# Hybrid decoder step on one core: projection stripes in another order, four projection banks, key rows turned by VectorE

## The chip, the cores and the metric

The kernel runs on one core of one Trainium2 chip. The metric is device time in microseconds, from the first to the last instruction of one execution with what lies around it; a smaller time is better. Times of before are of three runs, and one further execution was taken with the hardware profiler.

## What is computed

One layer of a decoder trunk is run on 1024 new prompt tokens and on 8 sampled tokens with caches, 1032 columns in all. Model width is 1024.

```python
xn = rms_norm(x, norm_pre)
u, z_rnn, q, k, v, z_attn, g_rnn, g_attn = split(xn @ w_in)       # 1024 -> 9216 columns
uc, conv_new = causal_conv(u, conv_buf, conv_w, conv_b)           # 4 taps
r, i = sigmoid(uc @ lru_w_a + b_a), sigmoid(uc @ lru_w_x + b_x)   # blocks of 64
a = exp(-8 * r * softplus(-lam))
h = scan(h = a * h + sqrt(1 - a * a) * i * uc)                    # over the tokens
y_rnn = (h * silu(z_rnn)) @ w_rnn_out
# three groups (window, dilation) = (128, 1), (512, 4), (2048, 16), 8 heads of 64 each
o_g, lse_g = dilated windowed attention with ALiBi per group      # sampled tokens read caches
y_attn = (merge of o_g by softmax(lse_g) * silu(z_attn)) @ w_attn_out
y = x + rms_norm((sigmoid(g_rnn) * y_rnn + sigmoid(g_attn) * y_attn) @ w_out, norm_post)
```

Outputs are y for both kinds of tokens, the convolution's and the recurrence's states, and the rows of k and v that the caches keep: of the prompt the last 128, 512 and 1024 positions of the three groups, for each of them 8 heads of 64 numbers.

## The kernel before

All products with weights are made of three passes in fp32r: each operand is split into a high part and a rest (`whi`, `wlo` and `xh`, `xl`; ScalarE makes the high part by a copy, VectorE the rest by a subtraction, L225 and L226), and `mm3` (L389) adds high x high, high x low, low x high. The normalised input lies in SBUF as 8 + 8 tiles [128, 1032]. `w_in` is used in 72 stripes of 128 columns, each loaded whole by SP (512 KB, L207). One stripe is one call of `project` (L409): three chunks of 256, 384 and 392 columns, each with 8 x 3 matmuls into a PSUM bank of the tag `pj`, which has two banks; then an eviction. The tags `s` (three banks), `pt` (two) and `o` (one) serve everything else.

Evictions: `proj_u` (L534) copies by ScalarE; `proj_z` (L545) and `proj_za` (L682) take Sigmoid by ScalarE and multiply by VectorE; `proj_g` (L1105) takes Sigmoid by ScalarE and then stores the tile to DRAM, after which its slot is free.

SBUF tiles come from `Arena`: 42 slots of one [128, 1059] tile, handed out first in, first out. If none is free, `get` calls `force`, which runs steps of the background lanes at once, whether due or not, until one is.

Work beside the projections stands in generators in lanes (`lru`, `attention`, `sample`, `merge`). The program is written out in one order by a planner: `clk` counts the price of each PE instruction, `mm` (L138) charges it, and a generator yields the time after which it may go on. `advance` runs a stripe and calls `tick` after each half chunk; `tick` issues at most one step of each lane that is due. A lane runs its generators one after the other.

The recurrence is four chains (`chain`, L611), two 128-row blocks each, all in the lane `lru`. A chain's front (`chain_front`, L561) does the convolution, splits the result and makes the gates: 12 steps of two matmuls and two activations per chain, 1300 apart (L603). Then Tanh into a new tile, Exp, Sqrt, VectorE work, the scan (L641), and the product with z, which is stored.

Order of the stripes: the first four (u0 to u3) are computed in four chunks (`EARLY`), interleaved by hand (`half`, `turned`) with the normalisation of the four token groups, whose transposed tiles they need; the norm takes a Sqrt on ScalarE per group (L335). Then z0 to z3, u4, u5, z4, z5, u6, u7, z6, z7, four za stripes and six gate stripes. A chain starts when both its u stripes and its z stripes are done, except that the first starts with z0. Then for each of four pairs of heads and each of three groups v, k, q, after which `attention` (L788) and, per pair, `sample` (L966) are spawned. The remaining ten gate stripes run under the last attention; two stripes before their end all merged heads and samples must have been issued (`until`, L1223). Three output products follow.

In `attention`, six steps, `STEP` apart, per group and pair. At the third and fourth step `k_rows` (L766) turns the kept 128-column blocks of k (1, 4 or 8 of them) by PE transposes into a bank `s`, copies them out by VectorE (L779), and later stores them: `store_rows` (L735) writes one row of 128 numbers per token, 512 bytes a piece.

## Time and profile before

| | |
|---|---|
| median of three runs | 1291.03 us (1291.01 to 1292.82) |
| the profiled execution's own time | 1294.25 us |
| its span, first to last instruction | 1292.5 us |
| mean granted TensorE clock | 0.987 |
| PE busy | 1258.5 us, 97% |
| VectorE (DVE), ScalarE (ACT), GpSimd (POOL) busy | 604.6, 553.2, 221.9 us |
| DMA moved | 125.98 MB, 32% of 16 queues' time |

The engines work side by side, each in its own order; one instruction waits until what it reads is written and what it overwrites is read. Busy PE means that a matmul is under way; matmuls overlap, so the lengths of single ones add up to more than their time. The granted clock is a share of the full 2.4 GHz.

### The profile page before, as it was taken

The page shows a single profiled execution, that of the slowest core. Times are in us where ns is not written, and L with a number is a line of the kernel's source. Part 1 is how long each engine was busy: PE and PEld are TensorE (multiplying, and loading weights), DVE is VectorE, ACT ScalarE, POOL GpSimd, SP SyncE. Part 2 cuts the span into 40 slices and gives each one's busy share as a digit, 9 for nine tenths or more (in the row PEclk, how much of TensorE's full clock was granted, in tenths as well). Part 3 has the DMA queues.
Part 4 walks back from the last instruction along what each step waited for, and adds up shares of the span by engine and source line. Part 5 has one row for each costly group of instructions (what it writes and reads, how often), then busy time and mean ns, then how long its engine had stood idle before and what let it go on. Part 6 is the DMA issues. An engine that isn't in the chain of part 4 may idle for free.

```text
span 1292.5 us, 21498 instructions
## 1 busy us (share of the span) xinstructions
PE 1258.5 (97%) x8726; PEld 1209.8 (94%) x8726; DVE 604.6 (47%) x1323; ACT 553.2 (43%) x1231; POOL 221.9 (17%) x232
## 2 busy tenths in 40 slices
PE   8999999799999999999999999999999999999997
PEld 8999998789999989999999999999999999998997
DVE  5552472761574274544256324643345245554226
ACT  6536636445539744334334344333652331222222
POOL 5000221311220131150026001420026000002001
PEclk9999999899999999999999999999999999998999
DMA  7210130232330133632074016512365474223115
GB/s 234 67 33 17 33 99 17 71 125 69 100 112 5 49 96 108 165 84 66 17 212 120 25 42 164 135 50 66 97 189 154 137 260 150 66 66 99 33 67 197
DMA packets 149449, 125.98 MB, mean 97 GB/s; under 512 B 8873, under 2 KB 135305, under 8 KB 149342
## 3 DMA queue, kind: packets, MB, share of 16 engines
q1 hardware_dynamic: 149350, 124.61, 32.0%
q8 instruction: 69, 1.13, 0.4%
q14 instruction: 30, 0.25, 0.1%
HBM read 98.44 MB, written 26.21 MB: 96 GB/s over the span
## 4 chain that ended last, share of the span: by engine, by line
PE 87%; ACT 5%; DVE 5%; issue 1%; DMA 1%; POOL 0%; SPq 0%; DVEq 0%; ACTq 0%
PE ps_pj L146 75%; PE ps_s L146 5%; PE ps_o L146 3%; PE ps_s L150 3%; PE ps_pt L150 2%; ACT gate L601 1%; DVE wlo L226 1%; DVE tanh L641 1%; ACT whi L225 1%; DMA wraw<-in_w_in 1%; DVE ck L1057 1%; ACT gate L623 1%; ACT sq L627 0%; ACT P L823 0%; ACT L627 0%
## 5 line engine op out<-in xcount | busy, mean ns | idle before, releaser
L146 PE MATMUL ps_pj<-xh,whi 128*128 128x256 f32 (+3 forms) x1760 | 574.7, 327 | 12.1 <-DVE za L687 11.0
L146 PE MATMUL ps_pj<-xl,whi 128*128 128x256 f32 (+3 forms) x1760 | 560.4, 318 | 0.0
L146 PE MATMUL ps_pj<-xh,wlo 128*128 128x256 f32 (+3 forms) x1760 | 560.1, 318 | 0.0
L146 PEld LDWEIGHTS ps_pj<-xh,whi 128*128 128x128 f32 x1760 | 334.0, 190 | 21.0 <-DVE za L687 12.4
L146 PEld LDWEIGHTS ps_pj<-xl,whi 128*128 128x128 f32 x1760 | 334.0, 190 | 0.2
L146 PEld LDWEIGHTS ps_pj<-xh,wlo 128*128 128x128 f32 x1760 | 333.6, 190 | 0.0
L226 DVE TENSOR_TENSOR wlo<-wraw,whi 128x512 fp32r<-128x512 f32 x176 | 149.6, 852 | 320.0 <-ACT whi L225 314.0
L225 ACT ACTIVATE whi<-wraw 128x512 fp32r<-128x512 f32 x176 | 109.6, 625 | 3.9 <-DMA wraw<-in_w_in 1.9
L823 ACT ACTIVATE P<-P,stat 128x128 f32<-128x128 f32 (+1 forms) x192 | 84.3, 440 | 53.0 <-DVE stat L819 52.9
L146 PE MATMUL ps_pj<-wlo,mh 128*128 128x256 f32 (+1 forms) x288 | 80.6, 286 | 0.1
L146 PE MATMUL ps_pj<-whi,mh 128*128 128x256 f32 x256 | 73.3, 286 | 2.7 <-ACT whi L225 2.7
L146 PE MATMUL ps_pj<-whi,ml 128*128 128x256 f32 x256 | 73.2, 286 | 0.0
L716 ACT ACTIVATE qt<-ps_pj,qsc 128x384 f32<-128x384 f32 (+1 forms) x36 | 27.6, 766 | 81.5 <-PE ps_pj L146 79.6
L146 PE MATMUL ps_pj<-hzh,wlo 128*128 128x256 f32 (+2 forms) x192 | 61.4, 320 | 0.0
L146 PE MATMUL ps_pj<-hzl,whi 128*128 128x256 f32 (+2 forms) x192 | 61.4, 320 | 0.0
L146 PE MATMUL ps_pj<-hzh,whi 128*128 128x256 f32 (+2 forms) x192 | 61.3, 319 | 0.0
L1109 ACT ACTIVATE sg<-ps_pj 128x256 f32<-128x256 f32 (+2 forms) x48 | 22.0, 458 | 91.7 <-PE ps_pj L146 90.4
L819 DVE CUSTOM_DVE_ANT_0 P<-ps_s,base 128x128 f32<-128x128 f32 (+1 forms) x192 | 56.0, 348 | 8.5 <-PE ps_s L146 8.0
L840 ACT ACTIVATE PT<-ps_pt 128x256 f32<-128x256 f32 (+1 forms) x48 | 21.0, 437 | 91.0 <-PE ps_pt L150 90.9
L601 ACT ACTIVATE gate<-ps_s,par 64x256 f32<-64x256 f32 (+2 forms) x96 | 52.1, 543 | 16.0 <-PE ps_s L146 14.4
L838 DVE COPY PT<-ps_pt 128x512 f32<-128x512 f32 (+1 forms) x48 | 28.7, 597 | 54.1 <-PE ps_pt L150 54.1
L146 PEld LDWEIGHTS ps_pj<-wlo,mh 128*128 128x128 f32 (+1 forms) x288 | 52.3, 181 | 0.5 <-DVE wlo L226 0.4
(247 smaller groups left out, 1690.1 us busy)
## 6 DMA issues: line engine op xcount, KB each, us to landing
wraw<-in_w_in SPq DMA_DIRECT2D x72, 512.0 KB
ck<-in_cache_kv_w SPq DMA_DIRECT2D x24, 512.0 KB
sgd<-sg SPq DMA_DIRECT2D x16, 516.0 KB
sgl<-sgd SPq DMA_DIRECT2D x16, 516.0 KB
xin<-in_x_prompt SPq DMA_DIRECT2D x16, 512.0 KB
qb<-sd SPq DMA_DIRECT2D x12, 512.0 KB
fb<-fd SPq DMA_DIRECT2D x24, 256.0 KB
hzd<-uc SPq DMA_DIRECT2D x8, 516.0 KB
```

What stands on the lines that cost most here:

```text
L146: nc.tensor.matmul(out, lhsT, rhs, start=start, stop=stop)
L150: nc.tensor.transpose(out, in_, idn)
L225: nc.scalar.activation(hi[:, a:b], raw[:, a:b], AF.Copy)
L226: nc.vector.tensor_tensor(lo[:, a:b], raw[:, a:b], f32(hi[:, a:b]), op=OP.subtract)
L601: nc.scalar.activation(G[gate][rows, cs], p[at:at + 64, :n], AF.Sigmoid, bias=par[rows, b, 5 + gate:6 + gate])
L623: nc.scalar.activation(R[b], R[b], AF.Exp, scale=spk[:, 1, b:b + 1])
L716: nc.scalar.activation(dst, src, AF.Copy, scale=C["qsc"][:, g, hp:hp + 1])
L819: nc.vector.tensor_tensor_reduce(out=pt[:, h, :128 * n], in0=ps[h][:, off:off + 128 * n], in1=base, scale=-SLOPES[g][2 * hp + h] * DIL[g], ...
L823: nc.scalar.activation(pt[:, h, :128 * n], pt[:, h, :128 * n], AF.Exp, scale=-1.0, bias=st[:, g, 0, h, b:b + 1], accum_out=st[:, g, 1, h, ...
L838: nc.vector.tensor_copy(t, src)
L840: nc.scalar.activation(t, src, AF.Copy)
L1109: nc.scalar.activation(z[:, c0:c0 + n], p[:, :n], AF.Sigmoid)
```

## The change

The 28 early stripes (u, z, za and now eight gates) come in a new order, and the chains start with the second u of their pair; eight gate stripes remain late. While the early stripes and the last two gate stripes and everything behind run, the banks of the tag `pt` serve the projections too, in turn with `pj`. The planner charges n / 2.25 + 4 for an fp32r matmul. The gate steps are 1000 apart, and Tanh is written over the input gate's tile. `k_rows` turns the kept blocks of k by one VectorE transpose of 32x32 squares in place of PE transposes and copies, at the third step; a square row holds 32 numbers, so the store, four DMAs per tile, writes pieces of 128 bytes.

```diff
--- before.py
+++ after.py
@@ -24,13 +24,18 @@
 WIN = (128, 512, 2048)
 COL_U, COL_Z, COL_Q, COL_K, COL_V = 0, 1024, 2048, 3584, 5120
 COL_ZA, COL_GR, COL_GA = 6656, 7168, 8192
-UZ = ((COL_U, (0, 1, 2, 3)), (COL_Z, (0, 1, 2, 3)), (COL_U, (4, 5)), (COL_Z, (4, 5)), (COL_U, (6, 7)), (COL_Z, (6, 7)))
 EPS = 1e-6
 BIG = 1e30
 NSLOT = 42
 WARM = 40
-EARLY_GATES = 6
 GATES = [(kind, b) for kind in range(2) for b in range(8)]
+LATE_GATES = 8
+
+FIRST = [("u", 0), ("u", 1), ("g", 0), ("g", 1)]
+EARLY_BLOCKS = [("z", 0), ("z", 1), ("u", 2), ("u", 3), ("g", 2), ("g", 3),
+                ("z", 2), ("z", 3), ("u", 4), ("u", 5), ("g", 4), ("g", 5),
+                ("z", 4), ("z", 5), ("u", 6), ("u", 7), ("g", 6), ("a", 0),
+                ("z", 6), ("z", 7), ("a", 1), ("a", 2), ("a", 3), ("g", 7)]
 STEP = 3400
 SPARE = 5
 KY, VY = 3000, 4000
@@ -78,7 +83,13 @@
     ar = Arena(arena_pool, NSLOT)
     new = ar.get
 
+
+    wide, turns = [True], [0]
+
     def ps_tile(tag):
+        if tag == "pj" and wide[0]:
+            turns[0] += 1
+            tag = ("pj", "pj", "pt", "pt")[turns[0] % 4]
         bufs = {"pj": 2, "s": 3, "pt": 2, "o": 1}[tag]
         return psum.tile([128, 512], F32, tag=tag, bufs=bufs, name="ps_" + tag)
 
@@ -140,7 +151,7 @@
         for q in out.shape[1:]:
             n *= q
         if rhs.dtype == F32R:
-            clk[0] += n / 2.4 if n >= 256 else max(4 * n / 2.4, 107)
+            clk[0] += n / 2.25 + 4 if n >= 256 else max(4 * n / 2.4, 107)
         else:
             clk[0] += max(4 * n / 2.4, 214) * (0.75 if out.shape[0] == 64 else 1.0)
         nc.tensor.matmul(out, lhsT, rhs, start=start, stop=stop)
@@ -171,19 +182,19 @@
     w_ao = I["w_attn_out"][0].rearrange("(k p) c -> p k c", p=128)
     w_oo = I["w_out"][0].rearrange("(k p) c -> p k c", p=128)
     WL = []
-    for base, bl in UZ:
-        for b in bl:
-            WL.append(w_in[:, :, base + 128 * b:base + 128 * b + 128])
-    for hp in range(4):
-        WL.append(w_in[:, :, COL_ZA + 128 * hp:COL_ZA + 128 * hp + 128])
-    for kind, b in GATES[:EARLY_GATES]:
-        WL.append(w_in[:, :, (COL_GA, COL_GR)[kind] + 128 * b:][:, :, :128])
+    for what, i in FIRST + EARLY_BLOCKS:
+        if what == "g":
+            kind, b = GATES[i]
+            c = (COL_GA, COL_GR)[kind] + 128 * b
+        else:
+            c = {"u": COL_U, "z": COL_Z, "a": COL_ZA}[what] + 128 * i
+        WL.append(w_in[:, :, c:c + 128])
     for hp in range(4):
         for g in range(3):
             for base in (COL_V, COL_K, COL_Q):
                 c = base + g * 512 + hp * 128
                 WL.append(w_in[:, :, c:c + 128])
-    for kind, b in GATES[EARLY_GATES:]:
+    for kind, b in GATES[-LATE_GATES:]:
         WL.append(w_in[:, :, (COL_GA, COL_GR)[kind] + 128 * b:][:, :, :128])
     for s in range(4):
         WL.append(w_ao[:, :, 256 * s:256 * s + 256])
@@ -600,13 +611,12 @@
                     at = 64 * (gate ^ s)
                     nc.scalar.activation(G[gate][rows, cs], p[at:at + 64, :n], AF.Sigmoid,
                                          bias=par[rows, b, 5 + gate:6 + gate])
-                yield 1300
+                yield 1000
         ar.free(*xs)
         R[b], gi = G
         nc.gpsimd.tensor_tensor(x, x, gi, op=OP.mult)
-        t = T[b] = new([128, NT], F32, "tanh")
-        nc.scalar.activation(t, R[b], AF.Tanh, scale=spk[:, 0, b:b + 1])
-        ar.free(gi)
+        T[b] = gi
+        nc.scalar.activation(gi, R[b], AF.Tanh, scale=spk[:, 0, b:b + 1])
 
     def chain(j):
         bl = (2 * j, 2 * j + 1)
@@ -763,25 +773,34 @@
             step = bl[1] - bl[0] if len(bl) > 1 else 1
             later(3000, lambda: store_rows(g, hp, 1, vn[:, bl[0]:8:step], bl))
 
-    def k_rows(g, hp, i):
+    def k_rows(g, hp):
+
         bl = kept(g)
-        part = bl[4 * i:4 * i + 4]
-        if not part:
-            return
+        n = len(bl)
         kt = kts[g, hp]
-        if i == 0:
-            kns[g, hp] = new([128, len(bl), 128], F32, "kn")
-        kn = kns[g, hp]
-        p = ps_tile("s")
-        for q, b in enumerate(part):
-            tr(p[:, 128 * q:128 * q + 128], kt[:, 128 * b:128 * b + 128], ident)
-        n = len(part)
-        nc.vector.tensor_copy(kn[:, 4 * i:4 * i + n], p[:, :128 * n].rearrange("p (b c) -> p b c", b=n))
-        if 4 * i + n == len(bl):
-            def out():
-                store_rows(g, hp, 0, kn, bl)
-                ar.free(kns.pop((g, hp)))
-            later(3000, out)
+        kn = kns[g, hp] = new([128, n, 4, 32], F32, "kn")
+        step = bl[1] - bl[0] if n > 1 else 1
+        nc.vector.transpose(kn.rearrange("p b c j -> p b (c j)"),
+                            kt.rearrange("p (b x) -> p b x", x=128)[:, bl[0]:8:step])
+        o = kv_out[g]
+        off = o.offset + hp * 128
+
+        def out():
+            for a in range(4):
+                src = kn[32 * a:32 * a + 32]
+                at = off + 32 * a
+                if g == 0:
+                    ap, src = [[1024, 32], [32768, 4], [1, 32]], src[:, 0]
+                elif g == 1:
+                    ap = [[4096, 32], [1024, n], [131072, 4], [1, 32]]
+                    at += (bl[0] // 2) * 1024
+                else:
+
+                    ap = [[16384, 32], [1024, 2 * n], [524288, 2], [1, 32]]
+                    src = src.rearrange("p b (r c) j -> p (b r) c j", r=2)
+                nc.sync.dma_start(bass.AP(tensor=o.tensor, offset=at, ap=ap), src)
+            ar.free(kns.pop((g, hp)))
+        later(3000, out)
 
     stats = {}
 
@@ -875,8 +894,8 @@
                 values(pairs[i - 2])
             if i < 2:
                 v_rows(g, hp, i)
-            elif i < 4:
-                k_rows(g, hp, i - 2)
+            elif i == 2:
+                k_rows(g, hp)
             if i == 3:
                 ar.free(kts.pop((g, hp)), qts.pop((g, hp)))
             if i == 5:
@@ -1102,12 +1121,12 @@
 
     sgd = dram.tile([2, KB, 128, NT], F32, name="sgd")
 
-    def proj_g(kind, b):
+    def proj_g(kind, b, chunks=CHUNKS):
         z = new([128, NT], F32, "sg")
 
         def evac(c0, n, p):
             nc.scalar.activation(z[:, c0:c0 + n], p[:, :n], AF.Sigmoid)
-        yield from project(evac)
+        yield from project(evac, chunks)
 
         def spill():
             nc.sync.dma_start(sgd[kind, b], z)
@@ -1137,7 +1156,7 @@
     def turned(gi, k0=0):
         ahead[:] = [lambda k: k >= k0 and next(norm[gi], None)]
 
-    started = [proj_u(b, EARLY) for b in range(4)]
+    started = [proj_u(0, EARLY), proj_u(1, EARLY), proj_g(*GATES[0], EARLY), proj_g(*GATES[1], EARLY)]
 
     def half(i, n=1):
         for _ in range(n):
@@ -1189,20 +1208,12 @@
     clear_low_w()
     C = late_consts()
     spawn("lru", chain(0))
-    for b in range(4):
-        advance(proj_z(b))
-    spawn("lru", chain(1))
-    for j in (2, 3):
-        for b in (2 * j, 2 * j + 1):
-            advance(proj_u(b))
-        for b in (2 * j, 2 * j + 1):
-            advance(proj_z(b))
-        spawn("lru", chain(j))
+    for what, i in EARLY_BLOCKS:
+        advance({"u": proj_u, "z": proj_z, "a": proj_za}[what](i) if what != "g" else proj_g(*GATES[i]))
+        if what == "u" and i % 2:
+            spawn("lru", chain(i // 2))
     spawn("lru", state_out())
-    for hp in range(4):
-        advance(proj_za(hp))
-    for kind, b in GATES[:EARLY_GATES]:
-        advance(proj_g(kind, b))
+    wide[0] = False
     for hp in range(4):
         for g in range(3):
             for kind in (2, 1, 0):
@@ -1218,11 +1229,12 @@
         nc.sync.dma_start(t, sgd[kind, b])
         sgt[kind, b] = t
 
-    for i, (kind, b) in enumerate(GATES[EARLY_GATES:]):
-        if i == len(GATES) - EARLY_GATES - 2:
+    for i, (kind, b) in enumerate(GATES[-LATE_GATES:]):
+        if i == LATE_GATES - 2:
             until(lambda: len(merged) == 4 and len(sampled) == 4)
             spawn("split", split_ya())
-        if i == len(GATES) - EARLY_GATES - 3:
+            wide[0] = True
+        if i == LATE_GATES - 3:
             load_sg(0, 0)
             load_sg(0, 1)
         advance(proj_g(kind, b))
```

## Rows read from the trace of the kernel before

**Rows 1.** The profile's page: busy us, share, instructions of each engine.

```profile
PE 1258.5 (97%) x8726; PEld 1209.8 (94%) x8726; DVE 604.6 (47%) x1323; ACT 553.2 (43%) x1231; POOL 221.9 (17%) x232
```

**Rows 2.** Windows: start:end, length, busy (instructions) by engine, PEclk, DMA, GB/s.

```profile
160.00:192.00 32.00, 32.00 (x206) 32.00 (x206) 23.34 (x28) 11.63 (x21) 9.76 (x13) 1.00 0.33 100
192.00:224.00 32.00, 29.32 (x171) 27.95 (x170) 8.97 (x13) 20.46 (x37) 2.38 (x2) 0.95 0.06 17
224.00:256.00 32.00, 25.10 (x146) 24.37 (x144) 21.90 (x19) 15.42 (x20) 12.51 (x7) 0.89 0.21 64
256.00:288.00 32.00, 27.89 (x162) 27.25 (x163) 21.88 (x30) 12.73 (x21) 6.93 (x11) 0.95 0.39 135
288.00:320.00 32.00, 32.00 (x202) 32.00 (x201) 4.39 (x7) 17.76 (x35) 1.12 (x1) 1.00 0.14 50
```

**Rows 3.** Timeline of ACT: start, length, operation, count, idle before.

```profile
211.08 1.17 ACT L601 ACTIVATE gate<-ps_s,par 64x384 f32<-64x384 f32 x2 [1.28 <-PE ps_s L146]
...
213.62 9.13 ACT L601 ACTIVATE gate<-ps_s,par 64x392 f32<-64x392 f32 x16
```

**Rows 4.** Timeline of ACT: starts of recurrence chains, fourth chain's Sqrt.

```profile
72.56 1.27 ACT L573 ACTIVATE cv<-ext,par 128x1056 f32<-128x1056 f32 x1
...
175.36 1.27 ACT L573 ACTIVATE cv<-ext,par 128x1056 f32<-128x1056 f32 x1 [0.78 <-POOL ext L570]
...
362.26 1.27 ACT L573 ACTIVATE cv<-ext,par 128x1056 f32<-128x1056 f32 x1 [5.96 <-POOL ext L570]
...
448.77 2.02 ACT L627 ACTIVATE sq<-tanh 128x1032 f32<-128x1032 f32 x2
```

**Rows 5.** Windows around the fourth chain's Exp and Sqrt.

```profile
452.00:456.00 4.00, 2.42 (x14) 2.09 (x12) 4.00 (x13) 1.26 (x1) 0.00 (x0) 1.00 0.00 0
456.00:460.00 4.00, 3.14 (x20) 1.81 (x22) 3.62 (x9) 2.22 (x11) 1.16 (x1) 0.86 0.24 70
460.00:464.00 4.00, 4.00 (x31) 3.67 (x28) 2.77 (x9) 2.32 (x9) 1.21 (x1) 0.71 0.00 1
```

**Rows 6.** Lines by form: count, busy us, mean ns of one.

```profile
L641 DVE TENSOR_TENSOR_SCAN tanh<-gate,sq 128x1024 f32<-128x1024 f32 x8 | 27.1, 3391 | 0.0
...
L150 PE MATMUL ps_s<-ident,kt 128*128 128x128 f32 x52 | 9.7, 301 | 0.0
...
L633 DVE TENSOR_SCALAR gate<-tanh 128x1032 f32<-128x1032 f32 x8 | 7.6, 946 | 0.1
```

**Rows 7.** Timeline of PE: a series of eight transposes.

```profile
402.51 1.04 PE L150 MATMUL ps_pt<-ident,P 128*128 128x128 f32 x8
```

**Rows 8.** Windows of 2 us: recurrence weight loads; one key store.

```profile
38.00:40.00 2.00, 2.00 (x20) 2.00 (x19) 1.72 (x4) 1.63 (x4) 0.00 (x0) 1.00 0.43 97
...
464.00:466.00 2.00, 2.00 (x16) 2.00 (x15) 1.16 (x2) 0.94 (x2) 0.00 (x0) 1.00 0.46 129
```

**Rows 9.** Timelines of SP and ACT: a weight load, its conversion.

```profile
506.65 3.25 SPq L207 DMA_DIRECT2D wraw<-in_w_in  x1
...
537.23 0.62 ACT L225 ACTIVATE whi<-wraw 128x512 fp32r<-128x512 f32 x1
```

**Rows 10.** Timelines of ACT and PE at the start.

```profile
32.55 0.20 ACT L335 ACTIVATE rstd<-rstd 128x2 f32<-128x2 f32 x1 [0.90 <-DVE rstd L334]
...
59.31 1.28 ACT L504 ACT_TABLE_LOAD   x1
...
24.67 0.38 PE L146 MATMUL ps_pj<-xh,whi 128*128 128x256 f32 x1 [0.56 <-ACT ext L540]
...
35.19 0.38 PE L150 MATMUL ps_s<-ident,xin 128*128 128x128 f32 x2
```

**Rows 11.** Timelines of ACT and DVE in the late gates.

```profile
927.64 0.50 ACT L1109 ACTIVATE sg<-ps_pj 128x392 f32<-128x392 f32 x1 [0.25 <-PE ps_pj L146]
...
997.40 0.50 ACT L1109 ACTIVATE sg<-ps_pj 128x392 f32<-128x392 f32 x1 [8.01 <-PE ps_pj L146]
...
992.40 0.17 DVE L1068 TENSOR_TENSOR ys<-ys,zas 128x8 f32<-128x8 f32 x1
```

## The prediction

> **What bounds the kernel now.** I read the page first, then the span in windows, then the timelines of the windows that stand out. TensorE (PE) is busy for 97% of the span and VectorE and ScalarE for less than half [rows 1]. So only three things can move the end: matmuls that are no longer issued, idle time of PE, and time in which PE runs at the lower (1.2 GHz) of its two clock levels. The total hides where the idle time lies, so I cut the span into windows of 32 us. In the stage of the input projections a clean window holds 206 or 202 matmuls. Three neighbouring windows, 192 to 288 us, hold 171, 146 and 162, with PE busy for 29.32, 25.10 and 27.89 us and a granted clock of 0.95, 0.89 and 0.95 [rows 2]. The shapes are those of the clean windows, so the count measures the loss: three windows at the mean of 204 would hold 612, there are 479, and 133 / 204 x 32 = 20.9 us are gone. This is the largest hole behind the start.
>
> The timeline of ScalarE says what made it. The recurrence's gates are normally two activations at a time with a piece of projection between, as at 211.08. At 213.62 sixteen come without a break, 9.13 us [rows 3], so eight steps of the recurrence were issued back to back. The code has one reason for that: `new` found no free slot and pumped the background lanes. The count agrees. Of 42 slots 16 hold xh and xl and 2 the recurrence weights, and the weights of two blocks take 5 at least and 7 when loads run ahead, so 17 to 19 are left. At 213 us the second chain holds 10 (x, two split copies and two gates for each of two blocks), stripes u4 to u7 four, z2 to z7 six: 20 before the first za tile is asked for. The lane was then pressed through its VectorE part as well, and every eviction queued behind it.
>
> A second, smaller loss lies where the fourth chain's Exp and Sqrt fall between the attention's Exp: PE is busy for 2.42 and 3.14 of 4 us and the clock falls to 0.86 and 0.71 [rows 5]. That is 1.58 + 0.86 of idle time and 0.14 x 4 + 0.29 x 4 = 1.7 of clock, 4.2 us.
>
> **The order of the stripes.** The chains run one behind the other: 102.8 us lie between the start of the first and of the second (72.56 to 175.36), and the fourth starts at 362.26 [rows 4]. In the new order u and z of a pair come when a chain can use them, with gate stripes between, which need their slot only until their store. I count the new worst case: a chain in its gates 10, the next pair's u two, its own z two, the following z one or two, one gate or za tile waiting for its store: 16 or 17, against the 20 of before and 17 to 19 available. So the forced run goes, and its 20.9 us with it. With a chain running at its ordinary pace the clean windows show PE busy for 32.00 of 32 us with two banks [rows 2], so nearly nothing should remain; I leave 0.5. Gain **20.4 us**; bounds 10 (the lane is still pressed for half as long) and 20.9.
>
> Eight gate stripes in place of six are evicted early, and eight in place of ten late. That moves matmuls and issues none.
>
> **Four banks, the planner's price, the gate step of 1000, tanh into the input gate's tile.** Four banks let evictions be later by two chunks, which pays only where PE waits for a bank; in the clean windows it does not. The new price of a matmul (n / 2.25 + 4 ns in place of n / 2.4) lets every due time come some 8% earlier in real time. A chain then takes 102.8 - 12 x 0.3 (gate steps) - about 7 (8% of its planned waits) = 92 us. The fourth begins near 72.6 + 3 x 92 = 349, 13 us sooner, and its Sqrt, which came 86 us after the start [rows 4], falls near 430, still inside the attention. So the 4.2 us of the second loss stay in my sum; bounds 0 and -4.2. Tanh must now wait until POOL has multiplied by the gate that it overwrites. ScalarE's queue behind it holds evictions and conversions; the multiplication runs while the other block's last gate step is issued, and the four banks cover the rest. I take 0.
>
> **Key rows.** 52 PE transposes go [rows 6]. A series of eight takes 1.04 us [rows 7]; less the length of the last, 0.30, that is 0.106 us from one to the next, and 52 x 0.106 = **5.5 us**, all on PE, which never idles in that stage. Bounds 4 and 7. On VectorE the copies from PSUM become 32x32 transposes. The trace of before shows none; the nearest rows for 1024 columns from SBUF are 0.95 us (a plain tensor_scalar) and 3.39 us (the scan) [rows 6]. I take 1.1, near the plain one, since one element in gives one out. VectorE is off the path at 47% [rows 1], so 0; at the upper end each of the eight longer transposes could hold the next scores' eviction for up to 1 us, +6 in all with what follows.
>
> The stores become four per tile, 128 bytes a piece: 6656 pieces per pair of heads in place of 1664 of 512 bytes. One window with a key store alone moves 129 GB/s x 2 us = 504 pieces at a share of 0.46 of 16 queues, 29 ns of a queue each. The 256-byte loads of the recurrence weights move 758 pieces at 0.43, 18 ns each [rows 8]. So the longest store, 4096 pieces, takes 4.7 to 7.4 us in place of 1.9. SP issues it, and the weight and cache loads queue behind. A weight load is issued at 506.65 and its conversion starts at 537.23 [rows 9] (the same block, by counting loads and conversions back from the last): 30 us of slack. The cover holds until a store lasts that long. I take +1 for cache loads that reach the sampled rows late; bounds -2 and +6.
>
> A rule of the Trainium skill speaks against this edit: DMA: Bandwidth & Descriptors, Specifications, says that transfers under 512 bytes make the DMA read, modify and write. No row here shows it for writes; were a piece then two transfers of 29 ns, an estimate by that page, the longest store would be 14.9 us, still inside the 30 us, and the sum would be the same.
>
> **The start.** Two of the four stripes that run while x is normalised now end in Sigmoid, not Copy. Each change between Sigmoid and the norm's Sqrt costs ScalarE a table load of 1.28 us. The first comes before the second group's splits; the next before the third group's Sqrt at 32.55, whose engine had idled 0.90 us. That group's transposes start at 35.19, just when PE wants them. Two more banks take away the wait of 0.56 us at 24.67 [rows 10]. 1.28 + (1.28 - 0.90) - 0.56 = **+1.1 us**; bounds 0 (the loads find idle time) and 4 (the gap also lowers the clock).
>
> **Sum.** -20.4 - 5.5 + 1.0 + 1.1 = -23.8 us. From the profiled execution's own 1294.25 that is 1270.4. The median of the runs is 1291.03, 3.2 below it, so the forecast is 1267.2, say **1267**.
>
> **The rivals.**
> (a) Deeper: the fourth chain gets out of the attention's way and the start costs nothing: 1267 - 4.2 - 1.1 = 1262. For it: the chains start sooner. Against it: the fourth comes only 13 us sooner.
> (b) Slots run out elsewhere: the fourth chain (10), its z (2), q, k, v, the next v, and the attention's three tiles are 19 of 19 when the attention begins. Before had the same count there and shows no burst; if one comes it gives back half to all of 20.9: 1277 to 1288.
> (c) The late check comes too soon. The merged heads and the samples must be issued before the seventh late gate stripe in place of the ninth. The last sample's last operation ends at 992.40, and the sixth late stripe's last eviction starts at 997.40 (six such rows, the first at 927.64) [rows 11]. The margin is 5 us, plus what earlier due times give. If it is crossed PE waits for POOL and VectorE, about 8 us: 1275.
> (d) The other side: a 128-byte piece is so slow that the weights come late. By the slack of 30 us this needs 4096 x p / 16 > 30 us, p above 117 ns, four times the row; the gain is used up at 36 us, 141 ns. At 160 ns the store lasts 41 us, 11 us are lost for each of four pairs, and the time is 1267 + 44 = 1311, slower. For it speaks the rule above; against it, that 256-byte pieces cost less than 512-byte ones here.
> (e) The order does nothing because the burst had another cause: 1288.
>
> **How the numbers follow.** Forecast 58% (1264 to 1271), (a) 15%, (b) 13%, (c) 8%, (d) 4%, (e) 2%. The range, 1258 to 1281, leaves out (d), (e), and most of (b); its ends take in the -2 and -4.2 below and half of the hole above. What a measurement can tell is about 0.2%, 2.6 us. Faster by more: forecast, (a), (c) and nearly all of (b), with something held back for a cost not seen: 0.90. Within: 0.04. Slower: (d) and the unseen, 0.06.
>
> **What would show it.** In windows of 32 us the projections hold about 204 matmuls up to the first q, k, v, with PEclk 1.00. ScalarE shows no run of more than a few gate activations. The 52 transposes of kt are gone from PE, and twelve transposes stand on VectorE. The fourth chain's Sqrt still falls inside the attention. Table loads appear between 24 and 60 us. I am wrong if a burst of gate steps appears anywhere, if ScalarE's conversions wait for weight loads in the attention, or if PE idles near the sixth late stripe.

## The result, and the profile after

The changed kernel takes 1273.89 us (median of 4 runs, 1272.77 to 1276.46), the kernel before 1291.11 beside it: ratio 0.9866, 95% interval 0.9847 to 0.9885. It is faster by 17.2 us, where 23.8 had been forecast; 1273.9 lies inside the range of 1258 to 1281. The profiled execution is 1272.8 us with a span of 1271.0.

The page of the changed kernel, engines' busy time; beside [rows 1], PE has 52 instructions fewer and its share is 98%:

```profile
PE 1244.6 (98%) x8674; PEld 1197.8 (94%) x8674; DVE 610.6 (48%) x1319; ACT 550.0 (43%) x1230; POOL 220.3 (17%) x232
```

The windows of the changed kernel: the start, then those of [rows 2], then one in the late gates:

```profile
0.00:32.00 32.00, 27.78 (x205) 26.22 (x206) 20.13 (x45) 23.59 (x44) 17.90 (x86) 1.00 0.75 236
...
192.00:224.00 32.00, 32.00 (x201) 32.00 (x200) 3.90 (x7) 20.84 (x38) 5.26 (x2) 1.00 0.24 73
224.00:256.00 32.00, 32.00 (x206) 32.00 (x206) 22.58 (x23) 16.40 (x25) 10.26 (x6) 1.00 0.15 43
256.00:288.00 32.00, 32.00 (x208) 32.00 (x207) 21.79 (x27) 17.88 (x31) 4.00 (x10) 1.00 0.30 100
...
960.00:992.00 32.00, 27.57 (x160) 27.27 (x159) 14.29 (x10) 4.57 (x10) 21.59 (x9) 0.89 0.61 182
```

The hole is gone: 201, 206 and 208 matmuls where 171, 146 and 162 stood. A new one is there: 160 matmuls between 960 and 992 us, where PE is idle for 4.4 us and the granted clock is 0.89.

To see where time went I cut each trace where one of four operations of ScalarE begins, which all the kernels have: the first eviction of a key tile, the last of a query tile, the last of a gate stripe, and the last copy that makes the high part of the mixed output. This table is worked out from ScalarE's timelines, one profiled execution of each kernel, in us:

```
               to first   keys, q, v,  late    out-        tail   span
               key tile   attention    gates   projection
before           368.6      544.6      129.5    137.3     112.5  1292.5
after            368.3      542.3      112.1    137.1     111.2  1271.0
order_alone      377.5      543.4      111.4    137.4     112.4  1282.1
banks_alone      359.3      545.2      127.3    137.2     111.1  1280.1
two_banks        377.4      541.4      111.9    138.0     111.4  1280.1
keys_alone       368.3      544.9      126.9    137.1     111.1  1288.3
pe_keys          368.4      544.6      113.3    137.2     111.4  1274.9
whole_rows       368.4      540.3      112.9    137.1     109.5  1268.1
sg_later         370.7      541.7      112.4    137.2     111.2  1273.1
sample_later     370.4      541.9      104.3    137.1     112.2  1266.0
free_lrw         368.3      541.8      110.8    137.2     106.1  1264.2
old_price        372.8      541.6      104.8    137.2     111.1  1267.5
both             369.6      541.0      106.6    137.3     106.0  1260.5
both_spread      371.5      540.8      104.2    137.4     105.8  1259.7
```

The new order puts two gate stripes more into the first stage and two fewer into the late gates. A stripe takes 11.3 us of PE when nothing stalls, by its last evictions in the timeline of ScalarE of the changed kernel:

```profile
1000.04 0.50 ACT L1128 ACTIVATE sg<-ps_pj 128x392 f32<-128x392 f32 x1 [3.78 <-PE ps_pj L157]
...
1011.39 0.50 ACT L1128 ACTIVATE sg<-ps_pj 128x392 f32<-128x392 f32 x1 [1.91 <-PE ps_pj L157]
...
1022.73 0.50 ACT L1128 ACTIVATE sg<-ps_pj 128x392 f32<-128x392 f32 x1 [3.81 <-PE ps_pj L157]
```

With 22.7 us for the two, the changed kernel gained 368.6 + 22.7 - 368.3 = 23.0 us in the first stage and 2.3 in the attention, lost 112.1 + 22.7 - 129.5 = 5.3 in the late gates, and gained 1.5 after them: 23.0 + 2.3 - 5.3 + 1.5 = 21.5, the difference of the spans. The medians differ by 17.2 only, because the profiled execution of before stood 3.2 us above its median and that of after 1.1 below. The start is what varies: the first 32 us hold 205 matmuls here, 192 in **both** and 176 in **both_spread**, whose first stage has the same code. Less than 3 us in the first column can't be read from one profile. Counted from the first eviction of a z stripe, which leaves the start out, the first stage takes 294.4 us in the kernel before and 294.7 to 294.9 in the eight runs that have the changed kernel's first stage; order_alone takes 302.0, two_banks 301.6 and banks_alone 285.8.

### The profile page after: what moved, and what is told of

It reads as the page before. It is cut to its first block, busy times and chain, and to the rows that moved or that the text cites. A ratio compares the mean times of both kernels' runs of the same rounds, so it can differ in the third digit from the quotient of the medians.

```text
span 1271.0 us, 21444 instructions
## 1 busy us (share of the span) xinstructions
PE 1244.6 (98%) x8674; PEld 1197.8 (94%) x8674; DVE 610.6 (48%) x1319; ACT 550.0 (43%) x1230; POOL 220.3 (17%) x232
## 5 line engine op out<-in xcount | busy, mean ns | idle before, releaser
L157 PE MATMUL ps_pj<-xh,whi 128*128 128x256 f32 (+2 forms) x1384 | 452.9, 327 | 0.0
L157 PE MATMUL ps_pj<-xl,whi 128*128 128x256 f32 (+2 forms) x1384 | 440.8, 318 | 0.0
L157 PE MATMUL ps_pj<-xh,wlo 128*128 128x256 f32 (+2 forms) x1384 | 440.5, 318 | 0.3 <-DVE wlo L250 0.3
L157 PEld LDWEIGHTS ps_pj<-xh,whi 128*128 128x128 f32 x1384 | 260.9, 189 | 8.9 <-issue 8.2
L157 PEld LDWEIGHTS ps_pj<-xh,wlo 128*128 128x128 f32 x1384 | 260.9, 189 | 0.5 <-DVE wlo L250 0.5
L157 PEld LDWEIGHTS ps_pj<-xl,whi 128*128 128x128 f32 x1384 | 261.2, 189 | 0.1
L157 PE MATMUL ps_pt<-xh,whi 128*128 128x256 f32 (+3 forms) x376 | 117.9, 314 | 0.0
L157 PE MATMUL ps_pt<-xl,whi 128*128 128x256 f32 (+3 forms) x376 | 117.3, 312 | 0.0
L157 PE MATMUL ps_pt<-xh,wlo 128*128 128x256 f32 (+3 forms) x376 | 117.2, 312 | 0.0
L157 PEld LDWEIGHTS ps_pt<-xl,whi 128*128 128x128 f32 x376 | 70.7, 188 | 0.1
```

The lines of the kernel that those rows point to most:

```text
L157: nc.tensor.matmul(out, lhsT, rhs, start=start, stop=stop)
```

## The experiments

Each ratio is to the kernel before, run on the same chip. The changed kernel stands at 0.9866. Edits are to the changed kernel unless the text says otherwise.

### What closed the hole

**order_alone**: of the whole change the order alone.

```diff
-        if tag == "pj" and wide[0]:
+        if tag == "pj" and False:
...
-            clk[0] += n / 2.25 + 4 if n >= 256 else max(4 * n / 2.4, 107)
+            clk[0] += n / 2.4 if n >= 256 else max(4 * n / 2.4, 107)
...
-                yield 1000
+                yield 1300
...
-        T[b] = gi
-        nc.scalar.activation(gi, R[b], AF.Tanh, scale=spk[:, 0, b:b + 1])
+        t = T[b] = new([128, NT], F32, "tanh")
+        nc.scalar.activation(t, R[b], AF.Tanh, scale=spk[:, 0, b:b + 1])
+        ar.free(gi)
...
+            tr(p[:, 128 * q:128 * q + 128], kt[:, 128 * b:128 * b + 128], ident)
```

> Only the order of the stripes and of the chains' starts, and eight early and eight late gates; two banks, the planner's old price, gate steps of 1300, tanh in its own tile and the key rows by PE as before. If the order alone removes the forced run, the windows from 192 to 288 us hold about 204 matmuls each and the time falls by 20.9 us less what the later part loses (about 5 where the late gates hold two slots for gate tiles early): 1291 - 16 = 1275, between 1270 and 1281. If the four banks or the new price do it, a burst of gate activations is still there and the time stays above 1283.

Measured: 1282.12 us, ratio 0.9918 (0.9896 to 0.9940).

**two_banks**: everything but the four banks.

```diff
-        if tag == "pj" and wide[0]:
+        if tag == "pj" and False:
```

> The changed kernel with two projection banks throughout. If banks matter only where PE waits for one, which the clean windows do not show: within 2 us of the changed kernel, 1272 to 1276, with up to 1 us lost at the start. If the four banks carry the gain of the first stage, 1285 or more, with PE waiting for evictions between 70 and 360 us.

Measured: 1282.14 us, ratio 0.9920 (0.9905 to 0.9935).

**banks_alone**: the kernel before with four banks, on up to the first key tile and again in the tail.

```diff
+    wide, turns = [True], [0]
...
+        if tag == "pj" and wide[0]:
+            turns[0] += 1
+            tag = ("pj", "pj", "pt", "pt")[turns[0] % 4]
...
+    wide[0] = False
...
+            wide[0] = True
```

> The kernel before with four projection banks in the first stage and the tail, and nothing else of the change. In the kernel before, TensorE waited 11 us on the banks behind VectorE in the forced run and lost 20.4 us there with the clock. If four banks are enough to carry TensorE over a forced run, the hole at 192 to 288 us closes without any change of order: the stage before the first keys goes from 368.6 to 350 us and the kernel to 1270 to 1274. If they only take up short delays and the forced run is longer than they cover, the hole stays at about its size and the time at 1288 to 1292. Between the two, 1276 to 1286, both are needed in part.

Measured: 1282.57 us, ratio 0.9927 (0.9911 to 0.9943).

The windows of two_banks, which has the new order:

```profile
224.00:256.00 32.00, 29.85 (x187) 29.32 (x186) 18.39 (x19) 16.85 (x24) 8.47 (x5) 1.00 0.19 53
320.00:352.00 32.00, 30.40 (x187) 29.76 (x187) 21.87 (x25) 13.04 (x20) 11.63 (x8) 1.00 0.28 90
```

What PE waited for in the first 380 us of two_banks (total, times, longest), two lines, and ScalarE's timeline in its first short window:

```profile
PE ps_pj L157 <- DVE zs L561: 2.3, 3, 1.2
PE ps_pj L157 <- DVE za L697: 2.0, 3, 1.2
```

```profile
227.38 1.28 ACT L633 ACT_TABLE_LOAD   x1
228.68 2.21 ACT L633 ACTIVATE gate<-gate,spk 128x1032 f32<-128x1032 f32 x2
230.90 1.28 ACT L560 ACT_TABLE_LOAD   x1
232.19 0.50 ACT L560 ACTIVATE zs<-ps_pj 128x392 f32<-128x392 f32 x1
...
233.22 1.28 ACT L637 ACT_TABLE_LOAD   x1
234.52 2.02 ACT L637 ACTIVATE sq<-gate 128x1032 f32<-128x1032 f32 x2
236.56 1.28 ACT L560 ACT_TABLE_LOAD   x1
237.85 0.39 ACT L560 ACTIVATE zs<-ps_pj 128x256 f32<-128x256 f32 x1
```

The windows of banks_alone (PE only), and its row of ScalarE's timeline:

```profile
192.00:224.00 32.00, 29.33 (x171) 0.95 0.06 17
224.00:256.00 32.00, 27.23 (x153) 0.89 0.23 68
256.00:288.00 32.00, 31.96 (x206) 1.00 0.42 148
```

```profile
211.95 9.11 ACT L606 ACTIVATE gate<-ps_s,par 64x392 f32<-64x392 f32 x16
```

The two parts act on different losses, and within what one profile tells they add up. The order alone takes 368.6 + 22.7 - 377.5 = 13.8 us from the first stage, the banks alone 368.6 - 359.3 = 9.3, and together they took 23.0; counted from the first z eviction it is 15.1, 8.6 and 22.2. The medians of order_alone and two_banks fell between the two branches of their expectations, since neither part does it alone.

In banks_alone the sixteen gate activations still come in one run, so by the same reading the slots still run out; what the banks save is the backlog of evictions after it (256 to 288 us is full). PE's 11.0 us of waiting behind za are gone there, and 4.8 us behind weight splits stand in the hole that is left.

With the order and two banks the run of sixteen is gone, but PE still waits for a bank where a chain's Exp and Sqrt fall between the evictions of z and za stripes. In ScalarE's timeline Exp, Sqrt and the evictions' Sigmoid take turns, with a table load of 1.28 us at each change, so two evictions stand at 232.19 and 237.85, over five us apart. VectorE, which finishes the eviction and which the trace names, had itself been idle for 3.9 to 4.8 us, waiting for ScalarE. At the two places with such a sequence, 233 to 239 and 323 to 329 us, lie 3.8 of the 4.3 us of waiting above, and the windows of 187 matmuls are these two. In order_alone the longest such wait, 2.1 us at 351 us, stands behind the third chain's Sqrt. The changed kernel has the same sequence (its second Sqrt is at 230.84) and four banks, and its window holds 206.

With two banks, price, gate step, tanh's tile and key rows together are worth nothing measurable: two_banks and order_alone have the same time.

### What the key rows are worth

**keys_alone**: the kernel before with the key rows of the change (VectorE's transposes, and four stores of 128-byte pieces for each tile).

```diff
-            tr(p[:, 128 * q:128 * q + 128], kt[:, 128 * b:128 * b + 128], ident)
...
+        nc.vector.transpose(kn.rearrange("p b c j -> p b (c j)"),
+                            kt.rearrange("p (b x) -> p b x", x=128)[:, bl[0]:8:step])
...
+                nc.sync.dma_start(bass.AP(tensor=o.tensor, offset=at, ap=ap), src)
```

> The kernel before with the key rows turned by VectorE and stored in 128-byte pieces, nothing else. If 52 PE transposes at 0.106 us are all that it moves: 1291 - 5.5 = 1285.5. If the stores, which held SP for 7.4 us per 1024-column tile, delay cache and weight loads enough to make PE wait, half or more is given back: 1288 or above. If the wait of the transposes for a bank counted too, 1283.

Measured: 1290.93 us, ratio 0.9995 (0.9983 to 1.0006): nothing.

**pe_keys**: the changed kernel with the key rows of before, the reverse of that diff.

> The changed kernel with the key rows turned by TensorE again and stored as before; order, banks, price and step stay changed. By the prediction's own sum the 52 transposes are worth 5.5 us to the stage of keys, queries and values: it would go from 542.3 to about 548 us and the kernel to about 1279. Rival: as in the run with the key rows alone, the time that TensorE saves is lost again in waits of the same stage, so the stage stays at 542 to 545 and the kernel at 1273 to 1276. Third: the small pieces cost more than the transposes save, 1270.

Measured: 1278.23 us, ratio 0.9902 (0.9888 to 0.9916).

**whole_rows**: VectorE turns, but the tile is stored in 512-byte pieces. It leaves out the order of the words: within the key rows they don't stand where the reference has them, so it only serves to measure.

```diff
-            for a in range(4):
-                src = kn[32 * a:32 * a + 32]
...
-                nc.sync.dma_start(bass.AP(tensor=o.tensor, offset=at, ap=ap), src)
+            store_rows(g, hp, 0, kn.rearrange("p b c j -> p b (c j)"), bl)
```

> The changed kernel with the key tile turned by VectorE as before, but each tile stored in 512-byte pieces, so the words within the key rows do not stand in the reference's order. If SyncE's long hold on the small pieces (7.4 to 7.6 us for a 1024-column tile) is what gives the saved TensorE time back, the stage of keys, queries and values gets 2 to 5 us shorter (538 to 540) and the kernel comes to 1269 to 1272. If it is VectorE's turning, or neither, the stage stays at 541 to 544 and the kernel at 1273 to 1276.

Measured: 1272.02 us, ratio 0.9849 (0.9832 to 0.9866).

VectorE's transposes in the changed kernel, lines by form (count, busy us, mean ns):

```profile
L783 DVE STREAM_TRANSPOSE kn<-kt 128x1024 f32<-128x1024 f32 x4 | 5.0, 1241 | 0.0
L783 DVE STREAM_TRANSPOSE kn<-kt 128x512 f32<-128x512 f32 x4 | 2.8, 707 | 0.0
```

SyncE's timeline around one store of a 1024-column key tile, in the changed kernel and then in whole_rows:

```profile
645.81 7.59 SPq L801 DMA_DIRECT2D out_kv_p<-kn  x4
653.50 0.68 SPq L1014 DMA_DIRECT2D qb<-sd  x1
654.27 0.64 SPq L1007 DMA_DIRECT2D ck<-in_cache_kv_w  x1
```

```profile
645.80 3.91 SPq L757 DMA_DIRECT2D out_kv_p<-kn  x2
649.81 0.58 SPq L1002 DMA_DIRECT2D qb<-sd  x1
650.49 0.94 SPq L995 DMA_DIRECT2D ck<-in_cache_kv_w  x1
```

In the stage of the attention pe_keys takes 544.6 us, the changed kernel 542.3, whole_rows 540.3. So the transposes are worth 4.3 us where the pieces stay whole, and by these two profiles the small pieces give 2.0 back. The 2.0 are a hint only: three other runs with the small pieces and the same code take 541.7 to 541.9, and the intervals of the changed kernel and whole_rows overlap. A store of four calls holds SyncE twice as long as one of two, 7.59 us against 3.91, and the cache loads behind it are issued 3.7 us later. The transposes themselves take 1.24 us, near the 1.1 of the estimate, and the trace shows nobody waiting for them. In the old order the stage did not get shorter at all (544.9 against 544.6); PE there waited 4.4 us for the softmax's P before its transposes (2.3 in the kernel before, 1.0 in the changed one) and 1.5 for the denominators. Why the two orders differ in that was not tried.

### What the late gates lost

Two views of the changed kernel show the jam: VectorE's timeline (start, length, idle before), then POOL's.

```profile
960.02 2.01 DVE L237 TENSOR_TENSOR wlo<-wraw,whi 128x512 fp32r<-128x512 f32 x1 [0.53 <-ACT whi L236]
972.14 1.58 DVE L237 TENSOR_TENSOR wlo<-wraw,whi 128x512 fp32r<-128x512 f32 x1 [10.11 <-DMA sgd<-sg]
973.65 3.42 DVE L1076 TENSOR_TENSOR ck<-ck,ck 128x1024 f32<-128x1024 f32 x1
976.99 2.88 DVE L237 TENSOR_TENSOR wlo<-wraw,whi 128x512 fp32r<-128x512 f32 x1
979.80 3.35 DVE L1076 TENSOR_TENSOR ck<-ck,ck 128x1024 f32<-128x1024 f32 x1
```

```profile
966.05 7.13 POOL L963 TENSOR_TENSOR ot<-ot,fb 128x1024 f32<-128x1024 f32 x3 [0.32 <-DMA fb<-fd]
973.13 2.85 POOL L965 TENSOR_TENSOR ot<-ot,ot 128x1024 f32<-128x1024 f32 x1
976.07 3.26 POOL L966 TENSOR_TENSOR ot<-ot,ot 128x1024 f32<-128x1024 f32 x1
979.41 2.67 POOL L968 TENSOR_TENSOR ot<-ot,zal 128x1024 f32<-128x1024 f32 x1
```

And PE's timeline, where it stops:

```profile
983.30 3.45 PE L157 MATMUL ps_s<-one,ck 128*128 128x1 f32 x16 [4.43 <-DVE ck L1076]
```

VectorE does nothing from 962.0 to 972.1. Its next instruction is a weight split; ScalarE makes the first half of it (whi) only at 967.98, behind two evictions, and from then on the trace names the store of a gate stripe (sgd), whose slot the split is to write. The last group's two additions stand behind the split in VectorE's program, though POOL has their products by 965.7. And PE's program puts the group's closing sums ahead of the next stripe's matmuls, so PE stops for 4.4 us, and the granted clock of the window is 0.89: by estimate 0.11 x 32 = 3.5 us more. Four kernels tried the links of this.

**sg_later**: the two gate stripes that come back from memory are fetched two stripes later, so two slots more are free.

```diff
-        if i == LATE_GATES - 3:
+        if i == LATE_GATES - 1:
```

> The changed kernel with the first two stored gate tiles loaded two late stripes later. Theory one: their two slots make the late part short of slots, so that the weight conversion at 962 us gets the slot of a gate tile still being stored and VectorE stands for 10.1 us; then that wait is gone and the time falls by 4 to 6 us, to about 1269. Rival: the late loss comes from the key store that holds SP and delays the gate tile's store; then the wait stays and the time is that of the changed kernel within 2 us.

Measured: 1274.75 us, ratio 0.9862 (0.9844 to 0.9880), late gates 112.4, PE's wait 4.2: no change. These two slots are not the cause.

**sample_later**: the last group's sums on PE come later in the plan.

```diff
-        yield 3000
+        yield 9000 if hp == 3 else 3000
```

> The changed kernel with the last sample group's closing sums on TensorE put 9000 instead of 3000 ns after their last addition. If the late gates lose because TensorE's program reaches these sums before VectorE has made the addition (4.4 us of waiting and the clock drop behind it), the wait goes, the late gates shrink from 112.1 to 106 to 108 us and the kernel comes to 1268 to 1271. If VectorE's own delay (10 us before a weight split) is the cause, TensorE runs into the split's weights instead, and the time stays within 1.5 us of the changed kernel's.

Measured: 1265.42 us, ratio 0.9795 (0.9781 to 0.9809), late gates 104.3; both went below what I expected. VectorE's and PE's timelines of sample_later:

```profile
973.85 1.64 DVE L237 TENSOR_TENSOR wlo<-wraw,whi 128x512 fp32r<-128x512 f32 x1 [10.06 <-DMA sgd<-sg]
```

```profile
985.37 1.84 PE L157 MATMUL ps_s<-one,ck 128*128 128x1 f32 x16
```

VectorE still stands for 10 us, and it costs nothing: PE works through its stripe, and the 16 sums take 1.84 us without a wait. The loss was the place of the sums in PE's program, 7.8 us.

**free_lrw**: the slots of the two recurrence weights are freed after the last chain.

```diff
+    def free_lrw():
+        ar.free(*lrw)
+        yield 0
+
+    spawn("lru", free_lrw())
```

> The changed kernel with the two slots of the recurrence's weights freed after the last chain. If the late jam comes from too few slots (the weight split at 972 us waits for a spilled gate stripe's store), VectorE's 10 us wait goes, TensorE's wait for the sums with it, and the kernel comes to 1268 to 1271 with late gates of 106 to 108 us. If slots are not the cause, late gates of 111 to 113 us and 1273 to 1276.

Measured: 1266.27 us, ratio 0.9806 (0.9790 to 0.9821). The time is below the 1268 to 1271 of my expectation, and the reason was another: VectorE's wait for the store is gone, but the late gates only shrink to 110.8 (PE still waits 2.1 us for the sums). The rest comes from the tail, 111.2 to 106.1. There the chain of waits of the changed kernel passes through an output weight that is loaded late (PE waits 2.5 us for its high part), and PE's window is short; then the same window of free_lrw, whose chain has no such load:

```profile
1158.42 3.35 DMA wraw<-in_w_out
```

```profile
1152.00:1184.00 32.00, 29.12 (x213) 0.95 0.35 115
```

```profile
1152.00:1184.00 32.00, 32.00 (x260) 1.00 0.31 100
```

The kernel before has that loss too (tail 112.5).

**old_price**: the planner's old price of a product.

```diff
-            clk[0] += n / 2.25 + 4 if n >= 256 else max(4 * n / 2.4, 107)
+            clk[0] += n / 2.4 if n >= 256 else max(4 * n / 2.4, 107)
```

> The changed kernel with the planner's old price of a product (its columns over 2.4 GHz). The higher price makes the same planned delay cover about 9% less of TensorE's work: from the last group's weights to its closing sums 19.6 us in the changed kernel, 23.0 before. If the price is what brings the sums before VectorE's additions, that distance grows to 21 us or more, TensorE's wait of 4.4 us falls to under 3 and the kernel comes to 1270 to 1273. If the price does nothing of note there, as the prediction had it, the wait stays at 4 to 5 us and the time at 1273 to 1276; if it pays elsewhere, as in the first stage, the old price costs 1 to 4 us.

Measured: 1268.88 us, ratio 0.9836 (0.9822 to 0.9851). What PE waited for, one line of old_price:

```profile
PE ps_s L157 <- DVE ck L1076: 0.2, 1, 0.2
```

Late gates 104.8, and the sums are where they were before, 22.7 us after the group's weights (967.26 to 989.97; 23.0 before; 19.6 when PE reached them in the changed kernel). The last addition ends 22.6 us after the weights in old_price, 22.9 before and 23.8 in the changed kernel. So in this kernel the new price is what brought the sums ahead of the additions: about 3 of the 4.4 us are the sums' earlier place, about 1 the later additions. The price does not only cost. From the first z eviction to the last query eviction old_price takes 839.8 us, and the changed kernel, sg_later and sample_later, which share their code up to there, 836.5 to 837.1; so the new price seems to earn about 3 us before the late gates, and loses 7.3 in them. It is not the only thing that can jam this stage: order_alone has the old price and still takes 111.4 us there, by a wait of 3.8 us for a bank.

### The edits that helped, together

**both**: sample_later and free_lrw.

> The changed kernel with both edits: the last group's closing sums 9000 ns after its last addition, and the recurrence's two slots freed. If the two remove different losses (the sums' wait in the late gates, 112.1 to 104.3; a shortage of slots at the tail, 111.2 to 106.1), they add: late gates about 104, last stage about 106, kernel 1258 to 1262. If both remove the same loss, 1264 to 1267.

Measured: 1262.69 us, ratio 0.9784 (0.9766 to 0.9802); late gates 106.6, tail 106.0. That lies just outside the first branch: most of the two gains add.

**both_spread**: also, a key tile's four stores 3000 ns of the plan apart.

```diff
-        def out():
-            for a in range(4):
+        def out(a):
...
-        later(3000, out)
+        for a in range(4):
+            later(3000 + 3000 * a, lambda a=a: out(a))
```

> The kernel with both edits, and a key tile's four stores issued 3000 ns of the plan apart instead of together. If SyncE's hold of 7.4 to 7.6 us on a 1024-column tile is what the small pieces cost (2 us in the run with 512-byte pieces), the stage of keys, queries and values comes to 540 or 541 us and the kernel 1 to 2 us under the one with both edits. If the pieces cost through the queues they fill and not through SyncE's hold, no difference beyond 1 us.

Measured: 1258.80 us, ratio 0.9761 (0.9746 to 0.9777), the fastest of all. The single edits took 0.71% and 0.60% from the changed kernel's ratio, the two together 0.82%: the tail keeps its gain in full, but in the late gates PE now waits 1.8 us for a score of the last group. Spreading the stores did not shorten the attention (540.8 against 541.0). That does not show SyncE's hold in one piece as the cost of the small pieces, and does not rule it out either: **both** is already within 0.7 us of whole_rows there, and the calls of a 1024-column tile still came in two pairs, held 4.86 and 3.91 us near 930 us, not one by one. The late gates are 104.2 in place of 106.6: the last cache load is issued over 3.84 us, not 5.44, and PE's wait of 1.8 is gone. The intervals of the two kernels overlap, so this difference is a hint.

## Why the prediction was right, and where not

**The time.** 1273.9 is inside the range and 6.7 above the forecast. By the profiled executions the gain is 21.5 us against 23.8 forecast. Stage by stage: the first stage with the start 19.3 forecast, 23.0 measured; the keys 4.5 and 2.3; the late gates nothing, and a loss of 5.3; what follows nothing, and a gain of 1.5. That these differences come to no more than 2.3 us is in part luck. The other 4.3 us are the offset of profiled execution to median, which was 3.2 above in the kernel before and is 1.1 below here.

**The forced run: right cause, wrong share.** The order removes it and the first stage got 23.0 us shorter. But the order alone gives 13.8, not 20.4. The step that failed is "with a chain running at its ordinary pace the clean windows show PE busy for 32.00 of 32 us with two banks": those two windows hold no Exp or Sqrt of a chain (in the kernel before the Sqrts of the four chains stand at 146, 233, 334 and 449 us), and the new order puts z and za stripes beside them.

**Four banks: wrong.** "In the clean windows it does not" pay was true and beside the point. PE did wait for a bank, 11.0 us in all behind za, inside the hole that I had given whole to the order. Two lines of PE's waits in the kernel before:

```profile
PE ps_pj L146 <- DVE za L687: 11.0, 5, 4.9
PE ps_s L146 <- DVE ck L1057: 0.4, 1, 0.4
```

Banks alone are worth 9.3 us. The two errors, 6.6 too much and 9.3 too little, nearly cancel, and that is luck.

**The planner's price, valued at nothing: wrong.** I had followed the earlier due times only through the chains. For their starts that came out: 92 us a chain forecast, (346.25 - 71.76) / 3 = 91.5 measured. The starts of the changed kernel's chains, first and fourth, and the fourth's Sqrt, in ScalarE's timeline:

```profile
71.76 1.26 ACT L584 ACTIVATE cv<-ext,par 128x1056 f32<-128x1056 f32 x1
...
346.25 1.27 ACT L584 ACTIVATE cv<-ext,par 128x1056 f32<-128x1056 f32 x1 [2.65 <-POOL ext L581]
...
413.40 2.02 ACT L637 ACTIVATE sq<-gate 128x1032 f32<-128x1032 f32 x2
```

The same earlier due times also moved the samples' sums on PE, and there a wait of 0.4 us became one of 4.4.

**The second loss: wrong that it stays.** The Sqrt still falls inside the attention, and earlier than forecast (413 against 430). But the 4.2 us around the fourth chain's Exp and Sqrt are nearly gone, as these windows of the changed kernel show:

```profile
404.00:408.00 4.00, 3.37 (x20) 2.17 (x18) 2.55 (x10) 3.97 (x11) 0.00 (x0) 1.00 0.12 32
408.00:412.00 4.00, 4.00 (x33) 3.45 (x33) 2.38 (x10) 4.00 (x11) 0.00 (x0) 1.00 0.43 120
412.00:416.00 4.00, 4.00 (x38) 3.46 (x38) 0.90 (x3) 3.97 (x6) 0.00 (x0) 1.00 0.53 143
```

PE is idle for 0.63 us where it was for 2.44, and the granted clock stays at 1.00; PE is not idle for more than 0.3 us again before 496 us. To lie inside the attention is not enough for the loss; what else it needs was not tried. The gain does not show in the stage's length: PE waits there for things it had not waited for, 1.6 us for rows of v, 1.3 for the softmax's statistics, 0.8 for gates.

**Rival (c): its time came, by another way.** "PE waits for POOL and VectorE, about 8 us: 1275", with 8 in 100. PE did wait for VectorE, 4.4 us and, by estimate, 3.5 of clock, and the sign named for it, PE idle near the sixth late stripe, was there. The check itself was not crossed: the last sample's last operation ends at 987.6, the seventh late stripe starts near 1000. The margin of [rows 11] was the wrong one to look at. For each step on the background lanes that ends in a matmul the question is how long its operand has been ready; in the kernel before PE waits 0.4 us for the same additions, so there was no margin at all.

**Key rows: mechanism right, 5.5 against 4.3; the stores' price open.** The +1 was put on late samples; up to 2.0 seem to be lost in the attention. The pieces are not slow enough to hold up weights, so (d) did not come. By the packet records of the changed kernel a piece of 128 bytes takes 13.4 ns of a queue on the mean of 26624, under the 18 to 29 that I had taken, and one of 512 bytes 29.4. So the trace does not bear out the rule that the prediction cites: no small piece takes the time of two transfers. I had priced the pieces on the queues and left out SyncE, which the four calls of the store shown above hold for 1.9 us each on the mean. Whether that hold is what the small pieces cost stays open.

**The start:** +1.1 was not seen. The first 32 us hold 205 matmuls against 198, within what executions of the same code differ by. So both terms of (a) came in the main, without its time, because the late gates and the attention lost elsewhere. (b) and (e) did not come.

## What to carry to other kernels

A hole in the bound engine can have two owners: a forced run upstream, and too few buffers to ride over the backlog that it leaves. Remove one alone before giving the whole hole to it. And when a planner's price moves every due time, look at each step that puts work of the bound engine behind another engine: the one with no margin pays, and moving that one step (here 6000 ns later, 8 us) can be worth more than the price.

## What the runs showed of the hardware

VectorE's weight split takes 0.69 us at the median of 176 and up to 2.9 us; the additions 1.2 to 3.4. The long ones are those beside POOL. A split ends 0.55 us after a POOL operation has ended in all 16 cases that took over 1.2 us, and an addition 1.08 us after one in all six that took over 2.4. In the two timelines of the late gates this can be followed: 973.72 after 973.18, 977.07 after 975.98, 979.87 after 979.33, 983.15 after 982.08. These remainders are a little less than the operations take alone (0.69 and 1.2), so the two engines run in turn there, not side by side. The Trainium skill, SBUF — State Buffer, section on the two separate sides, says that a VectorE operation with two SBUF inputs and a GpSimd operation that reads SBUF take a shared pair of ports exclusively, for a whole instruction; the split and the addition have two such inputs, POOL's operations there read SBUF tiles, and the trace agrees with it.

A call of SyncE that stores a part of a key tile in 128-byte pieces takes between 346 and 2935 ns in the changed kernel, 627 at the median of 48. The longest stand where cache or weight loads were issued just before; no run here separates the number of pieces from what else was queued.
